# Second layer of a two-layer mixer kernel on one core: the pool half of the input projection taken on row differences

## The chip, the cores and the metric

The kernel runs on one core of one Trainium2 chip. The metric is the device time of one execution in microseconds (us), median of several runs. The engines are TensorE (PE in the profile; PEld are its weight loads), VectorE (DVE), ScalarE (ACT), GpSimd (POOL) and SyncE (SP), which issues the weight transfers.

## What is computed

Two layers act on 256 tokens (a grid of 4 rows of 64) with 2048 channels, all in float32. The first is a gated linear attention beside a short convolution. The second, which the change touches, is this (cut from the reference):

```
# layer 2: u = x * (1 + sc) + sh, with sc, sh, gt from w_ada
xp, gate = split(u @ w_in_o)                  # 2048 x 4096: a pool half and a gate half
xg = xp.reshape(4 rows, 64 columns, 2048)
z  = [window_mean_over_rows(g, w) - g for g, w in zip(4 groups of 512 channels, (2, 4, 8, 16))]
z  = [z_g @ w_pool[g] for each group] * pool_scale
y  = (z * silu(gate)) @ w_out_o
x  = layer_norm(alpha * x + gt * y)
```

With four rows only, the windows 8 and 16 cover all rows, so groups 2 and 3 both take the mean over the four rows minus the row. Every z is a combination of the differences of neighbouring rows.

## The kernel before

The tokens are two tiles of 128 (m = 0, 1). A float32 product is made of three products of parts: a weight tile w is split into a high part wh (ACT, line 153) and the rest wl (DVE, line 154), the activations likewise into u1h and u1l, and `mm3` (lines 189 to 193) adds uh·wh, uh·wl and ul·wh. Weights come in units of four contraction tiles by 512 columns, 1 MiB each, into four raw buffers in rotation; SP issues a load as soon as DVE has released the buffer (line 139). The split parts lie in four wh and four wl buffers, two units deep, which PE releases. `w_next` hands out the units in the order of the list `specs`, with loads two units and splits one unit ahead.

The second layer's input projection has eight blocks of 512 columns, four units each: x0 to x3 (the pool half, columns g*512) and g0 to g3 (the gate half, D + g*512). The order is x0, g0, p0, x1, g1, p1, x2, g2, p2, x3, g3, p3, where p is the group's 512x512 pool product, one unit. Each unit takes 4 contraction tiles x 2 token tiles x 3 products = 24 products of 128x512. After an x block, `pool_in` transposes it (zT, line 1200), forms z from sums of rows on DVE (lines 1208 to 1226) and splits it into zh and zl (lines 1230, 1231). After a p block DVE multiplies the sums in PSUM with the gate (line 1280), and `to_y1` transposes and splits the result (y1T, lines 1243 to 1248). The output projection (oacc) and the last normalisation follow.

Between the units runs background work. The gate gt of this layer is summed on DVE from 16 loads of w_ada (tile aacc, lines 528 and 530: four instructions a load), 0.55 steps a unit, and each fourth sum goes through a product with ones on PE (gtb, line 517). `x1_gen` applies the first normalisation's scale and shift to the residual (line 1171, eight instructions of 128x1024). The start of the layer is special: x0 goes token tile by token tile (`gemm_by_tile`), so that m = 0 is at work while the first layer's normalisation of m = 1 (`to_u1`, lines 1145 to 1157, tiles xr, xT, uf, u1h, u1l) still runs. Two units of x0 are split early; the other two lie in buffers of their own (swh, swl).

A scheduler turns this into one fixed order of instructions for each engine; each engine then works through its own order and waits where its next instruction is not ready.

Of the kernel before, what the change touches and what calls it, by code (L numbers as in the profile page):

```python
# [17 lines left out]
P = 128  # L18
# [31 lines left out]
TILE_1 = 4  # L50
# [11 lines left out]
def kernel(  # L62
# [96 lines left out]
    # units in the order of their use; loads and splits run ahead of the products  # L159
# [71 lines left out]
    # columns 2, 3: silu of c and c_ctx; a window of 32 columns puts them on the rows 0, 1 or 2, 3 of a product  # L231
# [5 lines left out]
    # columns of colT: see the rows above  # L237
# [26 lines left out]
    def mod_rows(k0, n):  # L264
        """scale (rows 0, 1 of each group of 32) and shift (rows 2, 3) of n channel tiles, summed over every fourth contraction tile"""
# [173 lines left out]
    def v_fill(nb, kt, nk):  # L439
        """a part of the values' contraction, for the gaps that the loads leave"""  # L440
# [34 lines left out]
    def ada_unit(layer, k0, n0):  # L475
        """four contraction tiles of the modulation's weights, two slots of two"""
# [26 lines left out]
    def ada_rows_gen(layer, dst, engs):  # L503
        """the gate of a layer, on every partition: products on DVE, the sum over the channels with ones"""
# [27 lines left out]
    def ada_cols_gen(layer, n0, dst, bias, one, engs, on_pe=()):  # L532
        """a section as channel columns: products on DVE, or on PE for the column blocks in on_pe"""
# [88 lines left out]
    def gemm_by_tile(groups, getu, done, budget=0.0, between=None, halves=False):  # L622
        """one token tile behind the other: the first one's sums are done while the second is at work"""
# [21 lines left out]
    # masks over (key j, query i) of a block of 32: m <= (j xor i) < 2 m  # L645
# [28 lines left out]
    def to_channels(nat, dst, use_act):  # L674
        """nat: two token tiles with 128 * n columns; dst(ct) for pairs of channel tiles"""
# [122 lines left out]
    def gla_gen(hp):  # L798
# [19 lines left out]
        def scores(xk, xq, flip=0):  # L818
            """keys of a block of 32 against the queries of the same block, or of its neighbour"""
# [52 lines left out]
        # chunk of 64 against the next one, tile of 128 against the other  # L872
# [108 lines left out]
    def rsqrt_act(v):  # L981
        """1 / sqrt(v + EPS): logarithm and exponential, then a Newton step"""
# [8 lines left out]
    def rsqrt(v, scale):  # L991
        """1 / sqrt(scale * v + EPS) on DVE: a seed from the exponent bits, then Newton steps"""
# [75 lines left out]
    def ln_blocks(src, order, getu, res, gt, budget, after, before=None, between=None, halves=False):  # L1068
        """sums of residual and projection and their statistics; after(m, tiles, mean, variance) when token tile m is done"""
# [58 lines left out]
    u1h, u1l = [], []  # L1128
# [8 lines left out]
    def to_u1(m, rt, mean, var):  # L1137
        rstd = rsqrt_act(var)
        ms = slice(m * P, (m + 1) * P)
        for nb in range(4):  # L1140
            if m == 0:
                u1h.append(slot([P, 4, SEQ], F32R, "u1h"))
                u1l.append(slot([P, 4, SEQ], F32R, "u1l"))
            r = rt[nb][:, m, :]
# [4 lines left out]
            uf = slot([P, 4, P], F32, "uf")  # L1149
# [44 lines left out]
    def pool_in(g, xp):
        X = slot([P, 4, SEQ], F32, "X1")
        for c2 in range(0, 4, 2):
# [4 lines left out]
            nc.scalar.activation(X[:, c2 : c2 + 2, :], pt, AF.Copy, scale=0.5 if g == 0 else 1.0)  # L1201
# [4 lines left out]

        if g == 0:
            tt(out=R(z, 0), in0=R(X, 0), in1=R(X, 0), op=ALU.subtract)
            tt(out=R(z, 1, 3), in0=R(X, 0, 3), in1=R(X, 1, 3), op=ALU.subtract)
        else:  # L1210
            sa = slot([P, 4, P], F32, "sa")
            a_, b_ = sa[:, :, 0:64], sa[:, :, 64:128]
            tt(out=a_, in0=R(X, 0), in1=R(X, 1), op=ALU.add)
            tt(out=b_, in0=R(X, 2), in1=R(X, 3), op=ALU.add)
# [120 lines left out]
```

## Time and profile before

| | us |
|---|---|
| median of 3 runs (1014.5 to 1016.17) | 1014.81 |
| span of the profiled execution | 1014.8 |
| first layer's last normalisation, second layer's first product | about 700 |
| second layer's input projection and pools | about 700 to 914 |
| output projection, up to PE's last product | 914 to 1003.6 |
| last normalisation and store | 1003.6 to 1014.8 |

The span of the profiled execution is the median, so differences in the trace can be set against the median as they are. An engine's busy time says little for PE, whose products overlap in the record; the distance from one start to the next is the better measure. A wait is put down to what ended it.

### The profile page before, as it was taken

How to read it: one execution, taken by the hardware profiler on the slowest of the kernel's cores; microseconds unless marked ns; L12 is line 12 of the kernel's file. 1: busy time of each engine (PE TensorE's matmuls, PEld its weight loads, DVE VectorE, ACT ScalarE, POOL GpSimd, SP SyncE). 2: the span in 40 equal slices, each digit the busy share in tenths (PEclk: the TensorE clock that was granted, in tenths of full speed). 3: DMA queues.
4: the chain of work that ended last, by engine and by line, in shares of the span. 5: the costliest groups of instructions: out<-in, count | busy, mean ns of one | idle time of the engine just before them, and what ended most of it. 6: DMA issues, size and time to landing. Idle time of an engine off the chain costs nothing.

```text
span 1014.8 us, 14425 instructions
## 1 busy us (share of the span) xinstructions
PE 973.4 (96%) x5718; PEld 768.6 (76%) x5718; DVE 801.4 (79%) x1161; ACT 463.3 (46%) x629; POOL 24.0 (2%) x55
## 2 busy tenths in 40 slices
PE   5899999999999999989999999999999999999995
PEld 4566666778878877877878788887888887778885
DVE  1555556989996999699999879987769968576676
ACT  2422214365684775336563444446554454454340
POOL 2000000000000000000000000000100001000000
PEclk9999999999999999999999999999999999999998
DMA  9987899667786676757767897984887888877532
GB/s 264 327 264 261 284 289 331 203 226 254 249 298 243 199 258 219 258 171 249 245 213 248 290 322 253 323 315 170 292 308 233 277 267 277 284 268 257 175 121 83
DMA packets 150373, 255.45 MB, mean 252 GB/s; under 512 B 5079, under 2 KB 46721, under 8 KB 150305
## 3 DMA queue, kind: packets, MB, share of 16 engines
q1 hardware_dynamic: 146592, 245.13, 72.3%
q0 software_dynamic: 2896, 8.72, 2.7%
q8 instruction: 45, 0.74, 0.3%
q10 hardware_dynamic: 816, 0.68, 0.3%
q14 instruction: 24, 0.19, 0.0%
HBM read 252.41 MB, written 2.10 MB: 251 GB/s over the span
## 4 chain that ended last, share of the span: by engine, by line
PE 43%; DVE 31%; DMA 19%; issue 4%; ACT 3%; SPq 0%; DVEq 0%; ACTq 0%
DMA raw<-in_w_ada_dram 16%; DVE wl L154 11%; DVE aacc L530 8%; PE oacc L191 5%; PE oacc L193 5%; PE oacc L192 5%; PE xacc L193 4%; PE xacc L192 4%; PE xacc L191 4%; PE ada L275 2%; PE kacc L191 2%; PE kacc L193 2%; PE kacc L192 2%; PE pr L402 1%; DMA raw<-in_w_in_e_dram 1%
## 5 line engine op out<-in xcount | busy, mean ns | idle before, releaser
L153 ACT CAST wh<-raw 128x1024 fp32r<-128x1024 f32 (+1 forms) x250 | 257.8, 1044 | 252.6 <-PE xacc L193 97.8
L154 DVE TENSOR_TENSOR wl<-raw,wh 128x1024 fp32r<-128x1024 f32 (+1 forms) x250 | 297.9, 1211 | 40.6 <-ACT wh L153 38.1
L530 DVE SCALAR_TENSOR_TENSOR aacc<-raw,sil,aacc 128x512 f32<-128x512 f32 x240 | 179.5, 748 | 42.6 <-DMA raw<-in_w_ada_dram 38.7
L191 PE MATMUL xacc<-wh,uxh 128*128 128x512 f32 x384 | 152.6, 397 | 0.0
L193 PE MATMUL xacc<-wh,uxl 128*128 128x512 f32 x384 | 151.8, 395 | 0.0
L192 PE MATMUL xacc<-wl,uxh 128*128 128x512 f32 x384 | 150.3, 391 | 0.1
L192 PE MATMUL xacc<-wl,u1h 128*128 128x512 f32 x240 | 94.4, 393 | 3.2 <-DVE wl L154 3.0
L191 PE MATMUL xacc<-wh,u1h 128*128 128x512 f32 x240 | 95.2, 397 | 0.8 <-ACT u1h L1156 0.8
L193 PE MATMUL xacc<-wh,u1l 128*128 128x512 f32 x240 | 93.7, 391 | 0.0
L192 PEld LDWEIGHTS xacc<-wl,uxh 128*128 128x128 f32 x384 | 72.1, 188 | 16.2 <-DVE wl L154 1.0
L193 PEld LDWEIGHTS xacc<-wh,uxl 128*128 128x128 f32 x384 | 72.2, 188 | 15.3 <-issue 0.2
L191 PEld LDWEIGHTS xacc<-wh,uxh 128*128 128x128 f32 x384 | 72.1, 188 | 15.5 <-ACT wh L153 0.5
L422 DVE TENSOR_TENSOR knat<-kacc,knat 128x512 f32<-128x512 f32 x64 | 42.8, 686 | 34.5 <-PE kacc L193 34.3
L192 PEld LDWEIGHTS xacc<-wl,u1h 128*128 128x128 f32 x240 | 45.1, 188 | 16.0 <-DVE wl L154 6.1
L191 PEld LDWEIGHTS xacc<-wh,u1h 128*128 128x128 f32 x240 | 45.1, 188 | 11.2 <-ACT u1h L1156 1.3
L193 PEld LDWEIGHTS xacc<-wh,u1l 128*128 128x128 f32 x240 | 45.1, 188 | 9.5 <-DVE u1l L1157 0.4
L286 ACT COPY arow<-ada 128x256 f32<-128x256 f32 (+1 forms) x9 | 3.1, 349 | 100.8 <-PE ada L275 100.8
L275 PE MATMUL ada<-raw,sil 128*32 128x256 f32 (+1 forms) x576 | 36.4, 382 | 10.8 <-DMA raw<-in_w_ada_dram 10.7
L191 PE MATMUL oacc<-wh,y1h 128*128 128x512 f32 (+1 forms) x120 | 45.5, 379 | 0.0
L193 PE MATMUL oacc<-wh,y1l 128*128 128x512 f32 (+1 forms) x120 | 45.0, 375 | 0.0
L192 PE MATMUL oacc<-wl,y1h 128*128 128x512 f32 (+1 forms) x120 | 45.0, 375 | 0.0
L275 PEld LDWEIGHTS ada<-raw,sil 128*32 128x32 f32 x576 | 17.3, 119 | 27.4 <-issue 12.6
(326 smaller groups left out, 1685.6 us busy)
## 6 DMA issues: line engine op xcount, KB each, us to landing
raw<-in_w_ada_dram SPq DMA_DIRECT2D x96, 1024.0 KB, 6.4
raw<-in_w_in_e_dram SPq DMA_DIRECT2D x54, 1024.0 KB, 5.7
raw<-in_w_in_o_dram SPq DMA_DIRECT2D x32, 1024.0 KB, 6.5
raw<-in_w_out_e_dram SPq DMA_DIRECT2D x16, 1024.0 KB, 7.0
raw<-in_w_out_o_dram SPq DMA_DIRECT2D x16, 1024.0 KB, 5.2
raw<-in_w_in_e_dram SPq DMA_DIRECT2D x18, 512.0 KB, 6.9
raw<-in_w_pool_dram SPq DMA_DIRECT2D x4, 1024.0 KB, 8.1
gt<-in_b_ada_dram POOLq DMA_DIRECT2D x8, 256.0 KB, 4.6
```

What stands on the lines that cost most here:

```text
L153: nc.scalar.copy(h, r[:, j : j + w, :])
L154: nc.vector.tensor_tensor(out=l, in0=r[:, j : j + w, :], in1=h.bitcast(F32), op=ALU.subtract)
L191: nc.tensor.matmul(out=acc, lhsT=uh, rhs=wh, start=start, stop=False)
L192: nc.tensor.matmul(out=acc, lhsT=uh, rhs=wl, start=False, stop=False)
L193: nc.tensor.matmul(out=acc, lhsT=ul, rhs=wh, start=False, stop=stop)
L275: nc.tensor.matmul(out=ps[32 * g : 32 * g + 32, :], lhsT=sil[:, kt, 2 - 2 * half : 34 - 2 * half], rhs=r[:, j, :], start=half == 0 and kt ...
L286: arow_ins.append(nc.scalar.copy(a[:, :nw], ps))
L402: nc.tensor.matmul(out=pr[32 * g : 32 * g + 32, :], lhsT=wr[:, kk, :], rhs=quad_u[kk // 2][:, kk % 2, :], start=True, stop=True,)
L422: nc.vector.tensor_tensor(out=dst, in0=acc, in1=dst, op=ALU.add)
L530: e.scalar_tensor_tensor(out=a, in0=r[j], scalar=sc, in1=a, op0=ALU.mult, op1=ALU.add)
```

## The change

A function `row_steps` runs after the first layer's normalisation. It forms the three differences of neighbouring rows of u (3 x 64 = 192 tokens), in tiles d, and splits them: dm0 and dm1 are the high part and the rest of the first two differences (128 tokens), dm2 holds the high part of the third difference in its first 64 tokens and its rest in the other 64. For this uf is kept whole (four tiles instead of eight short-lived ones).

An x block (`d_block`) now takes five products a contraction tile instead of six: dm0·wh, dm1·wh, dm0·wl into one accumulator, dm2·wh, dm2·wl into the other; the two halves of the latter are added after the transpose. `pool_in` forms z from the differences. The blocks stand in another order, written out in a list. A pool product that comes before its gate is copied out of PSUM by ACT (pooled) and multiplied when the gate is there. The whole program is instruction for instruction the same up to the normalisation at the start of the second layer. The diff, cut to its core:

```
-    for g in range(4):
-        if g == 0:
...
+    ODD = ("g0", "x0", "x1", "p0", "x2", "p1", "x3", "p2", "g1", "p3", "g2", "g3")
+    for s in ODD:
+        g = int(s[1])
+        if s == "g0":
             wide.update(len(specs) + i for i in WIDE_1)
-        block(W_O, g * 512)
-        block(W_O, D + g * 512)
-        block(W_P[g], 0, (0,))
+        if s[0] == "p":
+            block(W_P[g], 0, (0,))
+        else:
+            block(W_O, (D if s[0] == "g" else 0) + g * 512)
...
-            uf = slot([P, 4, P], F32, "uf")
+            uf = ufs[nb][:, :, ms]
...
+    def row_steps():
+        for nb in range(4):
+            if nb % 2 == 0:
+                dms.append([slot([P, 8, P], F32R, f"dm{i}") for i in range(3)])
+            dh, dl, dx = (t[:, 4 * (nb % 2) : 4 * (nb % 2) + 4, :] for t in dms[-1])
+            d = slot([P, 4, 192], F32, "d")
+            uf = ufs[nb]
+            nc.vector.tensor_tensor(out=d, in0=uf[:, :, 64:256], in1=uf[:, :, 0:192], op=ALU.subtract)
+            for hi, lo, src in ((dh, dl, d[:, :, 0:128]), (dx[:, :, 0:64], dx[:, :, 64:128], d[:, :, 128:192])):
+                nc.scalar.copy(hi, src)
+                nc.vector.tensor_tensor(out=lo, in0=src, in1=hi.bitcast(F32), op=ALU.subtract)
...
+    def d_block(n0, evac):
+        accs = [acc_bank("xacc") for _ in range(2)]
+        for q in range(4):
+            parts = w_next((W_O, 4 * q, 4, n0))
+            for j in range(4):
...
+                nc.tensor.matmul(out=accs[0], lhsT=dh, rhs=wh, start=f, stop=False)
+                nc.tensor.matmul(out=accs[0], lhsT=dl, rhs=wh, start=False, stop=False)
+                nc.tensor.matmul(out=accs[1], lhsT=dx, rhs=wh, start=f, stop=False)
+                nc.tensor.matmul(out=accs[0], lhsT=dh, rhs=wl, start=False, stop=l)
+                nc.tensor.matmul(out=accs[1], lhsT=dx, rhs=wl, start=False, stop=l)
...
         if g == 0:
-            tt(out=R(z, 0), in0=R(X, 0), in1=R(X, 0), op=ALU.subtract)
-            tt(out=R(z, 1, 3), in0=R(X, 0, 3), in1=R(X, 1, 3), op=ALU.subtract)
+            nc.gpsimd.memset(R(z, 0), 0.0)
+            nc.vector.tensor_copy(R(z, 1, 2), R(X, 0, 2))
+            tt(out=R(z, 3), in0=e2, in1=R(X, 3), op=ALU.add)
...
+            tt(out=e2, in0=e2, in1=R(X, 3), op=ALU.add)
...
+                stt(out=R(z, 0), in0=e1, scalar=2.0, in1=e2, op0=ALU.mult, op1=ALU.add)
+                stt(out=R(z, 0), in0=e0, scalar=3.0, in1=R(z, 0), op0=ALU.mult, op1=ALU.add)
+                for r, e in enumerate((e0, e1, e2)):
+                    stt(out=R(z, r + 1), in0=e, scalar=-4.0, in1=R(z, r), op0=ALU.mult, op1=ALU.add)
...
+            if g in gates1:
+                for m in range(2):
+                    tt(out=gates1[g][:, m, :], in0=accs[m], in1=gates1[g][:, m, :], op=ALU.mult)
+                later.append(lambda g=g: to_y1(g, gates1[g]))
+            else:
+                pooled[g] = slot([P, 2, 512], F32, "pooled")
+                for m in range(2):
+                    nc.scalar.copy(pooled[g][:, m, :], accs[m])
         else:
...
+            o_block(D + g * 512, gate_evac(g))
+            if g in pooled:
+                tt(out=gates1[g], in0=gates1[g], in1=pooled[g], op=ALU.mult)
+                later.append(lambda g=g: to_y1(g, gates1[g]))
```

Where the fixed orders move is seen at three places. The first is DVE at the end of the normalisation of m = 1. Before, after the rest u1l_3 of the third channel quarter come the splits of the two late units of the first block (raw_175 and raw_176):

```order
L1157 TENSOR_TENSOR u1l_1_5902<-uf_5_6047,u1h_1_5901 128x4x128
L1157 TENSOR_TENSOR u1l_2_5917<-uf_6_6060,u1h_2_5916 128x4x128
L1157 TENSOR_TENSOR u1l_3_5932<-uf_7_6073,u1h_3_5931 128x4x128
L1155 TENSOR_SCALAR uf_8_6086<-xT_8_6081,A1_5244,B1_5245 128x128
L154 TENSOR_TENSOR swl_9_6097<-raw_175_5977,swh_9_6096 128x1024
L154 TENSOR_TENSOR swl_10_6101<-raw_175_5977,swh_10_6100 128x1024
L1157 TENSOR_TENSOR u1l_4_5947<-uf_8_6086,u1h_4_5946 128x4x128
L154 TENSOR_TENSOR swl_11_6107<-raw_176_6104,swh_11_6106 128x1024
```

Changed, DVE at the same place (d_1 is the first quarter's difference; raw_177 and raw_178 are the first two units of x0, the second block now):

```order
L1175 TENSOR_TENSOR d_1_6092<-uf_1_5903 128x768
L1161 TENSOR_TENSOR u1l_2_5917<-uf_2_5918,u1h_2_5916 128x4x128
L1161 TENSOR_TENSOR u1l_3_5932<-uf_3_5933,u1h_3_5931 128x4x128
L1159 TENSOR_SCALAR uf_4_5948<-xT_8_6078,A1_5244,B1_5245 128x128
L153 TENSOR_TENSOR wl_159_6261<-raw_177_6140,wh_159_6260 128x1024
L1178 TENSOR_TENSOR dm1_1_6090<-d_1_6092,dm0_1_6089 128x512
L153 TENSOR_TENSOR wl_160_6265<-raw_177_6140,wh_160_6264 128x1024
L1161 TENSOR_TENSOR u1l_4_5947<-uf_4_5948,u1h_4_5946 128x4x128
L153 TENSOR_TENSOR wl_161_6269<-raw_178_6142,wh_161_6268 128x1024
L153 TENSOR_TENSOR wl_162_6273<-raw_178_6142,wh_162_6272 128x1024
L1178 TENSOR_TENSOR dm2_1_6091<-d_1_6092,dm2_1_6091 128x4x64
```

The late units of the first block have moved behind all of the row steps and behind two units of the next block.

The second place is DVE while PE is in x2: the product of gate 0 with the first pool product. Before, DVE comes to it between the next two splits after p0:

```order
L154 TENSOR_TENSOR wl_169_6415<-raw_185_6378,wh_169_6414 128x1024
L154 TENSOR_TENSOR wl_170_6419<-raw_185_6378,wh_170_6418 128x1024
L1280 TENSOR_TENSOR gate_1_6231<-pacc_1_6412,gate_1_6231 128x512
L154 TENSOR_TENSOR wl_171_6454<-raw_187_6422,wh_171_6453 128x1024
L1280 TENSOR_TENSOR gate_1_6231<-pacc_2_6413,gate_1_6231 128x512
```

Changed, DVE at that product: it stands behind three units of x2 (raw_192, raw_194, raw_195) and the z of the second group:

```order
L153 TENSOR_TENSOR wl_184_6748<-raw_195_6715,wh_184_6747 128x1024
L1255 SCALAR_TENSOR_TENSOR z_2_6632<-X1_2_6619 128x4x64
L1256 SCALAR_TENSOR_TENSOR z_2_6632<-X1_2_6619 128x4x64
L1257 TENSOR_TENSOR z_2_6632<-z_2_6632,X1_2_6619 128x4x64
L1259 TENSOR_SCALAR z_2_6632<-z_2_6632 128x4x64 x3
L533 SCALAR_TENSOR_TENSOR aacc1_14_6541<-raw_193_6646,sil_106,aacc1_14_6541 128x512
L1317 TENSOR_TENSOR gate_1_6121<-pacc_1_6583,gate_1_6121 128x512
L1268 TENSOR_TENSOR zl_2_6643<-z_2_6632,zh_2_6642 128x1024
```

PE reads that gate (y1T) inside x2's last unit.

The third place is the product gtb_6 with ones. Before, PE comes to it at the end of the first unit of g1:

```order
L193 MATMUL xacc_34_6873<-wh_188_6839,u1l_1_5902 128x512
L1243 MATMUL y1T_3_6910<-ident_79,gate_2_6652 128x128 x4
L1243 MATMUL y1T_4_6919<-ident_79,gate_2_6652 128x128 x4
L517 MATMUL gtb_6_6928<-aacc1_14_6560,ones_136 128x512
L191 MATMUL xacc_33_6872<-wh_189_6874,u1h_2_5916 128x512
```

Changed, PE inside the third unit of x3, and DVE at the last step of the sum aacc1_14 that this product reads:

```order
L1221 MATMUL xacc_33_6875<-wh_192_6914,dm0_2_6104 128x512
L1222 MATMUL xacc_33_6875<-wh_192_6914,dm1_2_6105 128x512
L1223 MATMUL xacc_34_6876<-wh_192_6914,dm2_2_6106 128x512
L520 MATMUL gtb_6_6907<-aacc1_14_6541,ones_136 128x512
L1224 MATMUL xacc_33_6875<-wl_192_6915,dm0_2_6104 128x512
```

```order
L153 TENSOR_TENSOR wl_193_6950<-raw_202_6918,wh_193_6949 128x1024
L153 TENSOR_TENSOR wl_194_6954<-raw_202_6918,wh_194_6953 128x1024
L533 SCALAR_TENSOR_TENSOR aacc1_14_6541<-raw_199_6803,sil_106,aacc1_14_6541 128x512
L1264 SCALAR_TENSOR_TENSOR z_3_6860<-X1_3_6847,z_3_6860 128x4x64
```

On DVE the step stands behind the split of x3's fourth unit (raw_202), while PE asks for it inside the third.

## Rows read from the trace of the kernel before

**Rows 1.** Page, span and part 1: engine busy us (share) x instructions.

```profile
span 1014.8 us, 14425 instructions
PE 973.4 (96%) x5718; PEld 768.6 (76%) x5718; DVE 801.4 (79%) x1161; ACT 463.3 (46%) x629; POOL 24.0 (2%) x55
```

**Rows 2.** Busy time by stretch: start:end length, engines, granted clock, DMA share, GB/s.

```profile
430.00:435.00 5.00, 1.37 (x7) 0.84 (x6) 4.48 (x20) 0.79 (x1) 0.00 (x0) 1.00 0.68 212
435.00:440.00 5.00, 5.00 (x16) 3.63 (x15) 4.42 (x7) 1.85 (x3) 0.00 (x0) 0.66 0.00 0
711.00:903.00 192.00, 188.95 (x847) 153.05 (x845) 148.78 (x180) 89.79 (x108) 9.59 (x18) 1.00 0.82 277
769.00:803.00 34.00, 33.49 (x151) 27.12 (x150) 32.87 (x40) 16.52 (x19) 1.06 (x2) 1.00 0.78 259
```

**Rows 3.** Waits of PE, 690 to 1015 us: total, times, longest.

```profile
PE xacc L192 <- DVE wl L154: 3.0, 5, 1.1
PE xacc L191 <- ACT u1h L1156: 0.8, 1, 0.8
```

**Rows 4.** Waits of PE, 430 to 440 us.

```profile
PE yT L965 <- DVE y L959: 3.6, 1, 3.6
```

**Rows 5.** Order of time on PE: start, us, what.

```profile
695.54 1.06 PE L1148 MATMUL xT<-ident,xr 128*128 128x128 f32 x8
...
708.47 0.50 PE L191 MATMUL xacc<-wh,u1h 128*128 128x512 f32 x1 [0.83 <-ACT u1h L1156]
...
711.60 0.39 PE L191 MATMUL xacc<-wh,u1h 128*128 128x512 f32 x1
711.83 0.39 PE L191 MATMUL xacc<-swh,u1h 128*128 128x512 f32 x1
712.05 0.39 PE L192 MATMUL xacc<-wl,u1h 128*128 128x512 f32 x1
...
967.63 0.39 PE L192 MATMUL oacc<-wl,y1h 128*128 128x512 f32 x1
...
969.89 0.39 PE L193 MATMUL oacc<-wh,y1l 128*128 128x512 f32 x1
```

**Rows 6.** Groups on DVE, 711 to 903 us: busy, mean ns, idle before.

```profile
L154 DVE TENSOR_TENSOR wl<-raw,wh 128x1024 fp32r<-128x1024 f32 x61 | 72.7, 1218 | 6.9 <-ACT wh L153 6.6
L530 DVE SCALAR_TENSOR_TENSOR aacc<-raw,sil,aacc 128x512 f32<-128x512 f32 x56 | 41.9, 749 | 25.4 <-DMA raw<-in_w_ada_dram 24.5
L528 DVE TENSOR_SCALAR aacc<-raw,sil 128x512 f32<-128x512 f32 x4 | 1.9, 486 | 10.7 <-DMA raw<-in_w_ada_dram 10.7
```

**Rows 7.** Order of time on DVE: back-to-back distances of each shape.

```profile
708.45 0.69 DVE L1157 TENSOR_TENSOR u1l<-uf,u1h 128x512 fp32r<-128x512 f32 x1
...
711.49 2.52 DVE L154 TENSOR_TENSOR swl<-raw,swh 128x1024 fp32r<-128x1024 f32 x2 [0.21 <-ACT swh L153]
...
733.11 0.42 DVE L1208 TENSOR_TENSOR z<-X 128x256 f32<-128x256 f32 x1
733.44 0.95 DVE L1209 TENSOR_TENSOR z<-X 128x768 f32<-128x768 f32 x1
...
740.92 2.35 DVE L154 TENSOR_TENSOR wl<-raw,wh 128x1024 fp32r<-128x1024 f32 x2
743.20 0.74 DVE L530 SCALAR_TENSOR_TENSOR aacc<-raw,sil,aacc 128x512 f32<-128x512 f32 x1
743.86 2.35 DVE L154 TENSOR_TENSOR wl<-raw,wh 128x1024 fp32r<-128x1024 f32 x2
749.03 3.11 DVE L530 SCALAR_TENSOR_TENSOR aacc<-raw,sil,aacc 128x512 f32<-128x512 f32 x4 [2.82 <-DMA raw<-in_w_ada_dram]
```

**Rows 8.** Waits of SP's load queue, 690 to 1015 us.

```profile
SPq L139 <- DVE wl L154: 175.2, 42, 9.1
```

**Rows 9.** Groups on ACT, 711 to 903 us.

```profile
L153 ACT CAST wh<-raw 128x1024 fp32r<-128x1024 f32 x63 | 65.6, 1052 | 62.9 <-PE xacc L193 49.2 <-issue 4.4 <-PE pacc L193 3.4
L1264 ACT COPY xp<-xacc 128x512 f32<-128x512 f32 x6 | 3.5, 584 | 5.7 <-PE xacc L193 5.7
```

More of the change, by code (lines that the diff above doesn't have):

```diff
@@ L1205, in R @@
             return t[:, :, 64 * r : 64 * (r + n)]
+        e0, e1, e2 = (R(X, r) for r in range(3))
+        ts = nc.vector.tensor_scalar
         if g == 0:
-            tt(out=R(z, 0), in0=R(X, 0), in1=R(X, 0), op=ALU.subtract)
-            tt(out=R(z, 1, 3), in0=R(X, 0, 3), in1=R(X, 1, 3), op=ALU.subtract)
-        else:
[L1211 to L1214, printed above, removed]
+            nc.gpsimd.memset(R(z, 0), 0.0)
+            nc.vector.tensor_copy(R(z, 1, 2), R(X, 0, 2))
+            tt(out=R(z, 3), in0=e2, in1=R(X, 3), op=ALU.add)
+        else:
+            tt(out=e2, in0=e2, in1=R(X, 3), op=ALU.add)
@@ L1236, in to_y1 @@
         yl = slot([P, 4, SEQ], F32R, "y1l")
-        y1h.append(yh)
-        y1l.append(yl)
+        y1h[g], y1l[g] = yh, yl
         for c2 in range(0, 4, 2):
@@ L1248, in to_y1 @@
                 stt(out=yl[:, cc, :], in0=pt[:, j, :], scalar=wcol, in1=hq.bitcast(F32), op0=ALU.mult, op1=ALU.subtract)
-    for g in range(4):
-        if g == 1:
-            bg.append(x1_gen())
-        xp = slot([P, 2, 512], F32, "xp")
-        rest, gaccs = (0, 1, 2, 3), None
-        if g == 0:
-            accs = [acc_bank("xacc") for _ in range(2)]
-            groups = [(W_O, 0, (0, 1, 2, 3), accs, True)]
-            if TILE_1 > 4:
-                gaccs = [acc_bank("xacc") for _ in range(2)]
-                groups.append((W_O, D, tuple(range(TILE_1 - 4)), gaccs, False))
-                rest = tuple(range(TILE_1 - 4, 4))
-            gemm_by_tile(groups, getu_1, lambda m, cs, end: nc.scalar.copy(xp[:, m, :], accs[m]), budget=B)
-        else:
-            o_block(g * 512, lambda m, a: nc.scalar.copy(xp[:, m, :], a))
-        later.append(lambda g=g, xp=xp: pool_in(g, xp))
-        gate = slot([P, 2, 512], F32, "gate")
-        def gate_evac(m, a):
-            last_silu[0] = nc.scalar.activation(gate[:, m, :], a, AF.Silu)
-        o_block(D + g * 512, gate_evac, rest, gaccs)
-        accs = [acc_bank("pacc") for _ in range(2)]
-        def getz(m, kt):
-            s = slice(m * P, (m + 1) * P)
-            return zs[g][0][:, kt, s], zs[g][1][:, kt, s]
-        gemm(w_pool[0, g], 0, (0,), range(2), getz, accs, budget=B)
-        for m in range(2):
-            tt(out=gate[:, m, :], in0=accs[m], in1=gate[:, m, :], op=ALU.mult)
-        later.append(lambda g=g, gate=gate: to_y1(g, gate))
@@ new lines, with gate_evac, f, getz @@
+    gates1, pooled = {}, {}
+    def gate_evac(g):
+        gates1[g] = slot([P, 2, 512], F32, "gate")
+        def f(m, a):
+            last_silu[0] = nc.scalar.activation(gates1[g][:, m, :], a, AF.Silu)
+        return f
+    for s in ODD:
+        g = int(s[1])
+        if s == "g0":
+            accs = [acc_bank("xacc") for _ in range(2)]
+            f = gate_evac(0)
+            gemm_by_tile([(W_O, D, (0, 1, 2, 3), accs, True)], getu_1, lambda m, cs, end: f(m, accs[m]), budget=B)
+        elif s[0] == "x":
+            xp = slot([P, 2, 512], F32, "xp")
+            d_block(g * 512, lambda m, a: nc.scalar.copy(xp[:, m, :], a))
+            later.append(lambda g=g, xp=xp: pool_in(g, xp))
+            if g == 0:
+                bg.append(x1_gen())
+        elif s[0] == "p":
+            accs = [acc_bank("pacc") for _ in range(2)]
+            def getz(m, kt):
+                c = slice(m * P, (m + 1) * P)
+                return zs[g][0][:, kt, c], zs[g][1][:, kt, c]
+            gemm(w_pool[0, g], 0, (0,), range(2), getz, accs, budget=B)
+            if g in gates1:
[4 more added lines that the diff above has]
+                pooled[g] = slot([P, 2, 512], F32, "pooled")
+                for m in range(2):
+                    nc.scalar.copy(pooled[g][:, m, :], accs[m])
+        else:
+            o_block(D + g * 512, gate_evac(g))
+            if g in pooled:
+                tt(out=gates1[g], in0=gates1[g], in1=pooled[g], op=ALU.mult)
+                later.append(lambda g=g: to_y1(g, gates1[g]))
```

41 lines of the change are left out of this document (21 added, 20 removed).

## The prediction, made before the changed kernel ran

> **What bounds the kernel now.** I read the page first, then the stretches of the second layer, then the waits of PE, then DVE. The page gives PE 96% of the span [rows 1]; that alone is not enough, since products overlap in the record. The measure is the distance between starts: from 967.63 to 969.89 us ten products of 128x512 start, 0.226 us each, with no gap [rows 5]. In the second layer's input projection (711 to 903 us) PE is busy 188.95 of 192 us at full clock [rows 2], and between 690 and 1015 us it waits only 3.8 us in all, of which 3.0 us are waits for a split wl on DVE [rows 3]. So PE sets the end, and a product taken from it should be worth 0.226 us. But the second engine is close behind: DVE is busy 148.78 of the same 192 us [rows 2], and 43 us of its idle time are waits: 36.1 us in front of aacc for loads of w_ada, 6.9 us in front of a split [rows 6]. SP waits 175.2 us for DVE to give raw buffers back, 42 times [rows 8], so loads start when DVE has finished a buffer, and DVE stands still when the next load has not landed. The five waits of PE for wl [rows 3] are the places where this loop already was no faster than PE. ACT is far from its limit: 89.79 of 192 us [rows 2], and 49.2 us of the idle time in front of its casts are waits for PE [rows 9].
>
> **What is removed.** The pool half has 4 blocks of 16 contraction tiles. Six products a tile are 384, five are 320: 64 products less, 64 x 0.226 = **14.5 us** off PE. Weights, loads and splits of weights are the same in number. That two accumulators alternate costs nothing by the trace: at 711.60, 711.83 and 712.05 us products into different accumulators start 0.225 us apart [rows 5].
>
> The Trainium skill (TensorE: Matmul & The Clock Gate, Part 2) gives the gap of back-to-back products of 512 columns as 215.7 ns at full clock. By that price the 64 products would be worth 13.8 us, 0.7 us less; the trace's own distance, 226 ns, is used here.
>
> **What is added.** On DVE, per channel quarter, one difference of 768 elements (0.95 us alone, about 0.87 back to back), a rest of 512 (0.69, about 0.60) and one of 256 (0.42, 0.33) [rows 7]: four times 1.8 us are 7.2 us. The new pool_in is about 1 us shorter in all: for the first group a copy of 512 and a sum of 256 replace 256 and 768 elements, for the second ten short steps replace nine, three of them cheap scalings; groups 2 and 3 are even. The gates come out even too. DVE gains about 6 us of work. ACT gets eight casts (four of 512, four of 256 elements) and six copies of 128x512 at 0.58 us [rows 9], some 7 us, hidden by its 102 us of idle time; if that cover went, each would delay a cast of weights by as much.
>
> **The start of the layer.** The order puts x0's first unit and the row steps in front of the late units of g0. PE resumes at 708.47 us with m = 1 [rows 5]; 24 products later, at 713.9, it wants the first differences, and 12 products after that, at 716.6, the first dm2. On DVE, from 711.5 us, when before it began swl_9 [rows 7], stand four splits (1.14 each), two 512s (0.60) and one 256 (0.33) up to the rest of dm2: 6.1 us, so 717.6. PE waits 1.0 us there, and a further 0.3 to 0.5 us at x0's second quad, whose differences follow on DVE at 719 to 720.3. I take **1.4 us**; the ends are 0 (DVE gets there as PE does) and 4 us (one more load or cast late).
>
> **The x stretch.** This term decides. From 711.5 us up to the last step of aacc1_14, which gtb_6 reads, DVE has in its order 40 splits x 1.14 = 45.4 us, 32 aacc at 0.66 to 0.78 [rows 7], 22.4 us, eight xr of the splits' shape, 9.1 us, and 16.4 us of small ones (row steps, z, zl, gates, y1l): 93.3 us. Without idle time it would be done at 804.8. PE has 414 products (93.6 us) and 32 transposes (1.06 us for eight [rows 5], 4.2 us) from 708.47 to gtb_6, and the 1.4 us: 807.7. So DVE has only 2.9 us to spare, against 93.3 of work. The gate product in front of y1T is the same case a little earlier: its first half falls at 711.5 + 70 = 781.7, PE arrives near 784. Every microsecond that DVE is idle beyond about 3 is lost on PE. In the stretch 769 to 803, where DVE had xr, z and splits to do at once, it was busy 32.87 of 34 us, idle 3.3% [rows 2]; over all of 711 to 903 it was idle 22.5%, much of it while PE set the pace. Over 93 us of work these give 3 and 27 us of idle time. The load here is nearer the first row, but the loads of w_ada go on, which in the first row were far ahead. I take 8 us, so PE loses 8 - 2.9 = about **5 us**; the ends are 0 and 24 us.
>
> A long wait has a second price. When PE waited 3.6 us at 430 us [rows 4], its granted clock was 0.66 over the next 5 us [rows 2], as if 3.4 of them ran at 1.2 instead of 2.4 GHz: 1.7 us. I count that **once**, with ends 0 and 3.4.
>
> **The rest.** From g1 on, units take PE 24 x 0.226 = 5.4 us again, the supply's pace of before. About half of the 3.0 us of waits for wl lay in units that are now in the x stretch, counted anew there; so **-1.5 us** (ends -3 and 0). The output projection is left as it is: [rows 3] lists all waits of PE up to the end, and none is in oacc. What is late next is DVE, not ACT or DMA: in 711 to 903 the DMA engines moved 277 GB/s at 0.82 of their time [rows 2].
>
> **Sum**, against the profiled execution, which is as long as the median: 1014.8 - 14.5 + 1.4 + 5 + 1.7 - 1.5 = 1006.9. I say **1006.9 us**, 0.8% less.
>
> **Rivals.**
> 1. The full gain. DVE is idle for no more than 3 us in the x stretch, as in 769 to 803. Then 1014.8 - 14.5 + 1.4 - 1.5 = 1000.2; with one short wait 1001 to 1003. For it: DVE ran 34 us on end almost without a gap [rows 2]. Against: the loads of w_ada stood between, and an aacc in DVE's order waits for its load in front of all splits behind it [rows 6].
> 2. The supply takes what PE gives. DVE idles 16 us (17%) in the x stretch, since a unit of x leaves the loop 20 x 0.226 = 4.5 us instead of 5.4. Then PE loses 13, the sum is 1014.8 - 14.5 + 1.4 + 13 + 1.7 - 1.5 = 1014.9: no change. For it: the five waits for wl already there at 5.4 us a unit [rows 3].
> 3. Slower. DVE idles as in the whole stretch, 22.5%, 27 us. PE then loses 24 in waits at the gate and gtb and in front of splits, at least two of them followed by half clock (3.4): 1014.8 - 14.5 + 1.4 + 24 + 3.4 - 1.5 = 1027.6. It decides from about 18 us of idle time on. For it: the row itself, over 192 us; against: that idle time arose while DVE's splits waited for ACT and ACT for PE, which a DVE that is behind does not do.
> 4. The products do not get cheaper in step, because dm2, a tile of two kinds of halves, or the alternation raises the distance: at 0.25 us instead of 0.226 the 320 products cost 7.7 us more, 1014.6. Rows 5 speak against it.
>
> The Trainium skill (TensorE: Matmul & The Clock Gate, HAM oscillation) describes kernels in which every group of products starts at half rate after a wait for data; by that rule each of rival 3's long waits would pay the second price, and the trace agrees once, with 0.66 after 3.6 us.
>
> **How the numbers follow.** Forecast (DVE idle for 4 to 12 us, 1003 to 1011) 0.62; full gain 0.15; supply takes it 0.12, spread over 1011 to 1015.5; slower 0.08; dearer products 0.03. A measurement of this kernel can tell about 0.2%, 2 us, from no change: faster is below 1012.8, slower above 1016.8. Faster: 0.62 + 0.15 + 0.05 of rival 2 + 0.01 = 0.83. Same: 0.07 + 0.02 = 0.09. Slower 0.08. The range reaches 1001.5 to 1013.5: it leaves out the best third of the full gain (0.05), the worst half of rival 2 (0.06) and rival 3 (0.08).
>
> **What would show it.** Right: about 5650 products on PE; a first x block's products at 0.226 us; a wait of PE of about 1 us for a row step near 717; waits for the gate or for aacc in front of y1T and gtb_6 of some microseconds in all; DVE busy over 85% between 711 and 810. The first g1 product should start near 827 us. Wrong: DVE idle there as before (rivals 2 and 3 show waits for wl at every unit of x), a distance above 0.23 us (rival 4), or a wait above 4 us at the late units of g0, where swl_9 and swl_10 come after all row steps. If the start costs more than 4 us, my walk through DVE's order is wrong there.

## The result, and the profile after

The changed kernel takes 1006.82 us (median of 6 runs, 1005.23 to 1012.59) beside 1017.53 us (1014.5 to 1019.9) for the kernel before on the same chip: a ratio of 0.9898, 95% interval 0.9875 to 0.9921. Timed a second time (last experiment below) it took 1009.77 beside 1017.04, 0.992 (0.9896 to 0.9945). The forecast was 1006.9 us. The total came out, closer than its terms: some of them were wrong, and 10 us were left in the kernel.

The page of the profiled execution, span and busy time by engine:

```profile
span 1004.1 us, 14346 instructions
PE 958.9 (95%) x5654; PEld 757.0 (75%) x5654; DVE 807.0 (80%) x1172; ACT 468.9 (47%) x643; POOL 24.4 (2%) x56
```

Against [rows 1] the 64 products are gone (5718 to 5654), DVE has 5.6 us more, and the span is 10.7 us shorter. But not all of that is the change. Up to the point where PE resumes with the second token tile (m = 1) in the second layer's first block, both programs do the same work. In [rows 5] that is at 708.47 us; here, in order of time on PE:

```profile
432.69 0.41 PE L968 MATMUL yT<-ident,y 128*128 128x128 f32 x2 [1.95 <-DVE y L962]
...
704.54 0.50 PE L190 MATMUL xacc<-wh,u1h 128*128 128x512 f32 x1 [0.83 <-ACT u1h L1160]
```

PE is there 3.9 us sooner. Of these, 3.4 come from one place: it waited 1.95 us instead of 3.63 [rows 4], and its clock did not fall, as the stretch shows (columns as in [rows 2]: the seventh column is the granted clock):

```profile
435.00:440.00 5.00, 5.00 (x24) 4.24 (x23) 5.00 (x11) 2.78 (x7) 0.00 (x0) 1.00 0.36 98
```

So I measure what follows by the **length of the layer**: span less the start of that product. Before: 1014.8 - 708.47 = 306.3 us; after: 1004.1 - 704.54 = 299.6, which is 6.8 us less, not 10.7 and not 14.5. Where the other 7.7 us went stands in the waits of PE from 690 to 1005 us (total, times, longest), to be read beside [rows 3]:

```profile
PE y1T L1279 <- DVE gate L1326: 3.3, 1, 3.3
PE xacc L1221 <- ACT wh L152: 2.5, 1, 2.5
PE y1T L1279 <- DVE gate L1317: 1.1, 1, 1.1
PE xacc L190 <- ACT u1h L1160: 0.8, 1, 0.8
PE xacc L1223 <- DVE dm L1178: 0.6, 1, 0.6
PE xacc L191 <- DVE wl L153: 0.4, 1, 0.4
PE gtb L520 <- DVE aacc L533: 0.3, 1, 0.3
PE pacc L191 <- DVE wl L153: 0.3, 1, 0.3
PE xacc L1224 <- DVE wl L153: 0.3, 1, 0.3
```

Without the 0.8 us that both kernels have, these are 8.8 us against 3.0 before, 5.8 us more. After the longest, the clock fell over 5 us:

```profile
880.00:885.00 5.00, 1.69 (x11) 1.19 (x10) 3.69 (x5) 1.82 (x2) 0.00 (x0) 1.00 0.57 188
885.00:890.00 5.00, 5.00 (x19) 4.01 (x17) 4.85 (x7) 1.78 (x4) 0.00 (x0) 0.66 0.77 249
```

That costs 0.34 x 5 = 1.7 us of products; 5.8 + 1.7 = 7.5 of the 7.7. Three waits make most of it.

**743 us.** ACT's cast stood 9.01 us in front of a load that SP had issued at 731.08 and that took 11.1 us. On POOL's queue six loads of `x1_gen`, 256 KB each, had been issued from 728.22 to 731.47, while SP's weight loads ran. Order of time on ACT, then on POOL, then a stretch (DMA share and GB/s are the last two columns):

```profile
742.26 1.99 ACT L152 CAST wh<-raw 128x1024 fp32r<-128x1024 f32 x2 [9.01 <-DMA raw<-in_w_in_o_dram]
```

```profile
728.22 0.54 POOL L1184 DMA_DIRECT2D row<-in_ln_g_dram  x1 [3.58 <-PE xacc L192]
...
731.47 0.54 POOL L1184 DMA_DIRECT2D row<-in_ln_b_dram  x1
```

```profile
735.00:745.00 10.00, 7.20 (x31) 5.34 (x30) 4.46 (x6) 2.02 (x3) 0.00 (x0) 1.00 1.02 371
```

The share alone is no proof: without the rows it is as high (experiment 9, 1.04 over the same stretch). What differs is whose bytes they are. From 728 to 743 us the rows took 1.57 MB (q0, POOL's queue) beside 3.53 of weights (q1, SP's); in experiment 9, 729 to 744 us, weights took all 5.24, and such a load landed in 7.2 us. Packets, MB and share of the 16 engines, changed kernel first:

```profile
q1 hardware_dynamic: 1782, 3.53, 64.0%
q0 software_dynamic: 480, 1.57, 37.2%
...
q1 hardware_dynamic: 2638, 5.24, 99.4%
```

The rows' 1.57 MB at 371 GB/s are 4.2 us by estimate, and the load took 3.9 us longer. (The Trainium skill, DMA: Bandwidth & Descriptors, Queues, rings and completion order, says that each DMA engine goes round the queues it has work for, a packet at a time. Experiment 9 fits that; no run here shows the packets in turn.) The rows are not the only condition. In experiment 4 they went out at the same times, but the load had been issued at 724.58 us instead of 731.08, and PE did not wait.

**785 us.** DVE has done the eight xr steps of the same generator, 1.22 us each, between 759 and 775 us, and the gate's product, which PE waits for, comes behind them:

```profile
766.32 3.49 DVE L1191 TENSOR_TENSOR xr<-xr,row 128x1024 f32<-128x1024 f32 x3
...
784.37 0.74 DVE L533 SCALAR_TENSOR_TENSOR aacc<-raw,sil,aacc 128x512 f32<-128x512 f32 x1
785.03 0.68 DVE L1317 TENSOR_TENSOR gate<-pacc,gate 128x512 f32<-128x512 f32 x1
```

**881 us.** DVE stands 4.46 us in front of a step of the gate sum whose load has not landed; a split and the gate's product, whose inputs ACT had finished at 880.8 and 877.2 us, are queued behind it:

```profile
881.28 0.75 DVE L533 SCALAR_TENSOR_TENSOR aacc<-raw,sil,aacc 128x512 f32<-128x512 f32 x1 [4.46 <-DMA raw<-in_w_ada_dram]
881.95 1.22 DVE L153 TENSOR_TENSOR wl<-raw,wh 128x1024 fp32r<-128x1024 f32 x1
883.08 1.22 DVE L1326 TENSOR_TENSOR gate<-gate,pooled 128x1024 f32<-128x1024 f32 x1
```

### The profile page after: what moved, and what is told of

It is laid out like the page before. It is cut to its first block, busy times and chain, and to the rows that moved or that the text cites. A ratio compares the mean times of both kernels' runs of the same rounds, so it can differ in the third digit from the quotient of the medians.

```text
span 1004.1 us, 14346 instructions
## 1 busy us (share of the span) xinstructions
PE 958.9 (95%) x5654; PEld 757.0 (75%) x5654; DVE 807.0 (80%) x1172; ACT 468.9 (47%) x643; POOL 24.4 (2%) x56
## 4 chain that ended last, share of the span: by engine, by line
PE 49%; DVE 29%; DMA 15%; issue 4%; ACT 2%; SPq 0%; DVEq 0%; ACTq 0%
DMA raw<-in_w_ada_dram 12%; DVE wl L153 10%; DVE aacc L533 7%; PE oacc L190 5%; PE oacc L191 5%; PE oacc L192 5%; PE xacc L192 5%; PE xacc L191 5%; PE xacc L190 5%; PE ada L274 2%; DMA raw<-in_w_in_o_dram 2%; PE kacc L190 2%; PE kacc L192 2%; PE kacc L191 2%; PE pr L405 1%
## 5 line engine op out<-in xcount | busy, mean ns | idle before, releaser
L190 PE MATMUL xacc<-wh,u1h 128*128 128x512 f32 x112 | 44.9, 401 | 0.8 <-ACT u1h L1160 0.8
L191 PE MATMUL xacc<-wl,u1h 128*128 128x512 f32 x112 | 44.7, 399 | 0.5 <-DVE wl L153 0.4
L192 PE MATMUL xacc<-wh,u1l 128*128 128x512 f32 x112 | 44.5, 397 | 0.0
L190 PE MATMUL kacc<-wh,uxh 128*128 128x512 f32 x64 | 26.8, 418 | 1.5 <-ACT uxh L397 1.5
L1221 PE MATMUL xacc<-wh,dm 128*128 128x512 f32 x64 | 25.7, 402 | 2.5 <-ACT wh L152 2.5
L190 PE MATMUL kacc<-wh,uch 128*128 128x512 f32 x64 | 26.4, 412 | 0.5 <-DVE knat L425 0.5
```

The source lines that it names most:

```text
L190: nc.tensor.matmul(out=acc, lhsT=uh, rhs=wh, start=start, stop=False)
L191: nc.tensor.matmul(out=acc, lhsT=uh, rhs=wl, start=False, stop=False)
L192: nc.tensor.matmul(out=acc, lhsT=ul, rhs=wh, start=False, stop=stop)
L1221: nc.tensor.matmul(out=accs[0], lhsT=dh, rhs=wh, start=f, stop=False)
```

## The experiments

All times are medians; the layer's length is from one profiled execution as above (two of one kernel differ by 0.7 us before and 2.4 us after). The scheduler orders DVE anew in each kernel, so an edit moves more than its own lines.

| kernel | us | ratio to before (95%) | layer, us | waits of PE that matter, us |
|---|---|---|---|---|
| before | 1017.5 | | 306.3 | wl 3.0 in five |
| before again | 1015.9 | 0.9996 (0.9979 to 1.0013) | 305.6 | wl 2.3 in five |
| changed | 1006.8 | 0.9898 (0.9875 to 0.9921) | 299.6 | 2.5, 1.1, 3.3 |
| changed again | 1009.8 | 0.9920 (0.9896 to 0.9945) | 297.2 | 2.2, 1.1, 2.9 |
| six products | 1023.6 | 1.0079 (1.0060 to 1.0099) | 311.7 | 3.4 at y1T, wl 2.4 |
| old order, five | 1005.9 | 0.9908 (0.9893 to 0.9924) | 297.5 | wl 2.5, zl 2.2 |
| quarter sum | 1001.3 | 0.9866 (0.9845 to 0.9886) | 293.9 | 3.1 at y1T, wl 1.3 |
| no row steps | 1009.6 | 0.9943 (0.9921 to 0.9966) | | 4.6 and 2.7 at y1T |
| rows late | 1008.3 | 0.9914 (0.9892 to 0.9936) | 297.7 | 4.4 and 2.0 at y1T |
| sum behind gate | 1004.7 | 0.9876 (0.9849 to 0.9903) | 292.4 | 2.1 at 746, 0.9 at y1T |
| gate first | 1007.2 | 0.9915 (0.9888 to 0.9943) | 299.5 | 2.9, and 3.7 at y1T |
| xr later | 1007.7 | 0.9899 (0.9870 to 0.9928) | 296.3 | 5.3 in two at y1T |
| three moves | 1003.5 | 0.9857 (0.9834 to 0.9880) | 293.6 | 3.2 at y1T |
| xr behind gate | 997.3 | 0.9800 (0.9775 to 0.9824) | 287.7 | none over 0.8 |

**1. Before again.** No edit.

> The kernel before, unchanged, profiled once more. In the two profiles so far the second half of the last output block of layer 1 resumes at 708.47 us (before) and 704.54 us (after), although both programs are the same up to there; the difference of 3.9 us lies at 430 us, where PE waited 3.6 us for y and then ran at a granted clock of 0.66 (before), against 2.0 us and full clock (after). Theory: that is chance, not the change; this profile shows either kind, a span between 1010.5 and 1015 us, and the timed runs stay at 1014 to 1020. Rival: the change reaches back in some way; then this profile shows 3.6 us and 0.66 at 430 again, and 708.5.

PE waited 2.58 us at 435.21 us, the clock stayed at 1.00, and the resume came at 706.74 us. Theory: part of the 10.7 us between the first two profiles is chance. In the thirteen profiles that have the row (the resume with m = 1) it lies between 704.2 and 710.4 us; the changed kernel alone has 704.5 and, profiled again, 710.3, and the kernel before lies between, at 708.5 and 706.7.

**2. Six products again**, order and row steps kept (the added product counts one term twice):

```
-                nc.tensor.matmul(out=accs[1], lhsT=dx, rhs=wl, start=False, stop=l)
+                nc.tensor.matmul(out=accs[1], lhsT=dx, rhs=wl, start=False, stop=False)
+                nc.tensor.matmul(out=accs[1], lhsT=dx, rhs=wh, start=False, stop=l)
```

> The changed kernel with a sixth product in each of the 64 contraction tiles of the pool half: the product of the third difference with the high part stands twice (its sum counts that term twice). Order, differences, splits and loads stay. Theory 1 (PE sets the end, and some 4 us of the waits in the x stretch, 2.8 at 743, 1.1 at 785 and 0.3 us for the gate's sum, come from DVE being short there): the 64 products cost 14.5 us and those waits go, so 10 to 14.5 us more than the changed kernel's 1006.8: 1017 to 1021. Rival (the x stretch runs at the pace of loads and splits, products are hidden in waits): 0 to 5 us more, 1007 to 1012.

The layer is 12.1 to 14.5 us longer than the changed kernel's two (311.7 less 299.6 or 297.2): theory 1, PE sets the end, and the 64 products are worth nearly all of their 14.5 us. The median, 1023.6, is above the 1017 to 1021 expected, 16.8 and 13.8 us above the changed kernel's two medians. One part of theory 1 failed: the wait at the gate, 1.1 us in the changed kernel, did not go but grew to 3.4 us (at 793.29 us), with clocks of 0.68 and 0.63 over 790 to 800 us. The second finding: with as many products as before the layer is 5.4 to 6.1 us longer than before's two. That is the price of the new order and the row steps.

**3. Old order, five products**, no differences:

```
+        if five[0] and m == 1:
+            nc.tensor.matmul(out=acc, lhsT=uh, rhs=wh, start=start, stop=False)
+            nc.tensor.matmul(out=acc, lhsT=uh, rhs=wl, start=False, stop=stop)
+            return
...
+        five[0] = n0 < D
         gemm(W_O, n0, quads, range(2), getu_1, accs, first=first, budget=B)
+        five[0] = False
```

> The kernel before with its order of blocks and without any differences, but one of the six products of the pool half left out in all 64 contraction tiles (the low part of the second token tile, so that part of the sum is missing). It shows what the removal of products alone is worth. Theory 1: PE sets the end and DVE has no row steps and no blocks of five products back to back, so 12 to 14.5 us come off the 1017.5 of before: 1003 to 1005.5, 2 to 4 us under the changed kernel; what the changed kernel lost against 14.5 us is then the price of its row steps and its order. Rival: the supply of split weights takes it in the old order too: 8 us or less, 1009.5 or more.

The edit reached three blocks of the pool half only, 48 products and not 64, since x0 is written by another routine; 48 are worth 10.9 us. The layer became 8.1 to 8.8 us shorter; the median, 1005.9, is just above the 1003 to 1005.5 expected for 64. So the old order, without a row step, also lost 2 to 3 us, to a wait for zl and two for wl: part of the supply rival is true in either order.

**4. Quarter of the gate sum:** three of four steps are left out.

```
-                ada_accum(ada_unit(layer, k0, n0), k0, a, engs)
+                ada_accum(ada_unit(layer, k0, n0), k0, a, engs, 1 if layer else 4)
...
-            for j in range(4):
+            for j in range(n):
```

> The changed kernel with three of every four multiply steps of the layer-1 gate sum left out (48 of 64, some 33 us of DVE); the loads of w_ada stay. Theory 1 (DVE's work is what is short): the waits of PE for the gate at 785 and 881 us and for the gate's sum go, 5 to 8 us less: 999 to 1002. Rival (loads are short, not work): the first step of a unit still stands in DVE's order ahead of the gate and waits for its load, as 4.5 us at 877 to 881 us in the changed kernel; PE's waits at 743 and 881 us stay, 0 to 2 us less: 1005 to 1007.

The time is theory 1's, its mechanism is half wrong: the waits at 743 and 881 us went, but the one in front of the first y1T stayed and grew (at 781.81 us, 3.1 us):

```profile
PE y1T L1279 <- DVE gate L1317: 3.1, 1, 3.1
```

The gate's product came 4.1 us sooner than in the changed kernel (780.98 us, not 785.03), but PE asked for it 6.0 us sooner (778.8, not 784.8): the wait at 743 us was no longer ahead of it, and the xr steps still stood ahead of the gate, from 755 to 771 us.

**5. No row steps:** the five products read u1h and u1l.

> The changed kernel without the row differences: the five products of a tile read the tiles of layer 1's output as they are (so the pool half is not the differences' product), and DVE and ACT have none of the row steps, 7 us on DVE. Number and order of products, blocks, loads and splits stay. Theory 1 (the row steps push the splits of the late units of the first gate block back, buffers come free later, and the load that PE waits for at 743 us starts late): PE's waits at 713 (0.6 us) and 743 us (2.5 us) go, with the products' slow restart behind them some 4.5 us: 1002 to 1003 against 1006.8. Rival (the wait at 743 us comes from the order, six loads that share the DMA engines from 726 us on): it stays, and only the 1 us at 713 goes: 1005.5 to 1006.

Both missed. The wait at 743 us went, as theory 1 says, but the time is 1009.6, above the changed kernel's first median (1006.8) and level with its second (1009.8). PE now stood 4.58 us at the first y1T (795.37 us), with a clock of 0.83 over 790 to 800, and 2.66 us at a later one (895.15 us). This profile has no resume row; the eight xT ahead of it start at 702.33 us, against 691.63 and 697.35 in the changed kernel's two. From there to the end it is 311.0 us, against 312.5 and 310.2: no gain. By the same clock PE came to the first y1T 4.7 us sooner than in the changed kernel's first profile and the gate's product only 1.2 us sooner, so the same deadline was missed by more.

**6. Rows late:**

```
-    row_steps()
+    row_steps(0, 2)
+    later.append(lambda: row_steps(2, 4))
```

> The changed kernel with the row steps of channel quarters 2 and 3 written behind the first gate block and x0's first unit, so that the splits of the late gate units come first on DVE; nothing is left out. Theory 1 (as in the run without row steps): splits end some 3.5 us earlier, buffers come free earlier, PE's wait of 2.5 us at 743 us shrinks or goes: 2 to 3.5 us less, 1003 to 1005. Rival: the late differences hold up x0's third unit, a wait for a difference of 1 to 4 us takes the place: 1006 to 1009.

The wait at 743 us fell from 2.5 to 0.6 us, theory 1, and more than that came back at the first gate, which neither text had named (the median, 1008.3, is the rival's):

```profile
PE y1T L1280 <- DVE gate L1318: 4.4, 1, 4.4
```

After it the clock over 790 to 795 us was 0.51.

**7. Sum behind the gate:** the sum's steps are held over the last two units of g1 to g3 and issued behind the gate's product.

```
-        with prio(ADA_PRIO):
+        with prio(ADA_PRIO), (tc.issue_after(gate_ins[-1].ins) if gate_ins else nullcontext()):
...
+        held[0] = True
+        gemm(W_O, n0, HOLD[1], range(2), getu_1, accs, first=False, budget=B)
+        held[0] = False
```

> The changed kernel with the steps of the layer-1 gate sum held back over the last two units of g1, g2 and g3 and placed behind the gate's product on DVE; nothing is left out. Theory 1 (at 877 to 881 us DVE stood 4.5 us in front of a step of the sum whose load had not landed, with a split and the gate's product queued behind it, and PE waited 3.3 us for that, then ran at a granted clock of 0.83 over 880 to 890 us): both go, 4 to 5 us less, 1002 to 1003. Rival: the steps that come later hold up a split behind them; waits for wl of the same size appear after the gate, 1005.5 to 1008.

Theory 1: the wait at 881 us and the slow stretch went, no wait for wl took their place, and the layer is 292.4 us, 4.8 to 7.2 us shorter. The median, 1004.7 (998.0 to 1007.3), is above the 1002 to 1003 expected; it carries the scatter from before the layer, and the waits at 746 and 789 us stayed.

**8. Gate first:**

```
+                with prio(-GATE_PRIO):
+                    for m in range(2):
+                        tt(out=gates1[g][:, m, :], in0=accs[m], in1=gates1[g][:, m, :], op=ALU.mult)
```

> The changed kernel with the product of gate and pooled values moved ahead in DVE's order for g0 (by one or two splits and one step of the sum); nothing is left out. Theory 1 (the wait of 1.1 us in front of y1T at 785 us is DVE's order): it goes, 1 to 1.5 us less, 1005 to 1006. Rival (DVE is full there, busy 9.9 of 10 us): the wait moves to a split or to the gate's sum, within 0.5 us of the changed kernel, 1006.3 to 1007.3.

The rival's time with another mechanism: the wait at 785 us went; the one at 743 us (2.9 us) was followed by a clock of 0.66 over 745 to 750 us this time, which took the gain.

**9. xr later:**

```
-            if g == 0:
-                bg.append(x1_gen())
...
+            if g == 1:
+                bg.append(x1_gen())
```

> The changed kernel with the eight steps xr (residual times ln_g, plus ln_b; 9.1 us of DVE) written at g1 instead of behind x0; nothing is left out. In the changed kernel they stand on DVE from 759 to 775 us, ahead of the gate's product that PE waits for at 785 us. Theory 1 (what DVE has to do in the x stretch ahead of that gate decides the wait): with 9.1 us less there the wait in front of y1T goes, also in profiles where PE reaches it sooner, 1.5 us less by the changed kernel's profile and up to 5 us by the others': 1002 to 1005.5. The wait at 743 us stays. Rival (the gate waits for a chain of its own: product, cast, sum): the wait stays within 1 us of what it was, 1006 to 1008.

The wait at 785 us went, as theory 1 says; so did the one at 743 us, which it said would stay. The eight row loads of the same generator, 2 MB on POOL's queue, had moved with the steps, and the weight load issued at 732.03 us was there for the cast at 739.23, in 7.2 us instead of 11.1:

```profile
739.23 2.00 ACT L152 CAST wh<-raw 128x1024 fp32r<-128x1024 f32 x2 [4.99 <-DMA raw<-in_w_in_o_dram]
```

But the steps now stood ahead of g1's gate, and PE waited there, and again at the next one, so that the median, 1007.7, is the rival's:

```profile
854.15 1.06 PE L1279 MATMUL y1T<-ident,gate 128*128 128x128 f32 x8 [2.94 <-DVE gate L1326]
...
882.06 1.53 PE L1279 MATMUL y1T<-ident,gate 128*128 128x128 f32 x8 [2.33 <-DVE gate L1326]
```

**10. Three moves** (6, 7 and 9 together).

> Three moves together, nothing left out: xr steps at g1, row steps of channel quarters 2 and 3 behind the first gate block, steps of the gate sum behind the gate's product for g1 to g3. Theory 1 (the changed kernel's loss of 8 us against the pitch is three separate waits, at 743, 785 and 881 us with what follows each): PE's time beyond the pitch falls from 16.4 us to 8 to 10 us, as in the kernel before (8.5 and 7.8): 998 to 1001, the full 14.5 us. Rival (DVE is short over the whole layer and a wait that is cured comes back at the next place, as the run with late row steps shows at 790 us): 1003 to 1006.

The rival's time (1003.5), and its mechanism too: the three waits went, but one came at the next place, 3.2 us in front of g1's y1T, behind xr; the layer is 293.6 us.

**11. xr behind the gate:** as 10, with `x1_gen` started at g2 and its steps queued behind g1's gate product on DVE; nothing is left out.

```
+                with tc.issue_after(gate_ins[0].ins):
+                    nc.vector.tensor_tensor(out=rt[nb], in0=rt[nb], in1=t.unsqueeze(1).to_broadcast([P, 2, 512]), op=op)
...
+            if g == 2:
+                bg.append(x1_gen())
```

> As the three moves together, but the xr steps stand behind g1's gate product on DVE instead of ahead of it; nothing is left out. In the run before, xr ahead of that gate made PE wait 3.2 us in front of y1T at 850 us and run slow after it, 5.1 us together. Theory 1 (each wait is a matter of what stands ahead of the gate in DVE's order): that goes, PE's time beyond the pitch falls from 10.6 us to 5 to 7 us: 998 to 1000. Rival (DVE has no room there either): a wait of 2 to 4 us comes at g2's gate or at a split, 1002 to 1005.

Theory 1, and more: 997.25 us (995.2 to 1000.31), 2.0% under the kernel before and the best here. PE's waits from 690 us on, and the two halves of the layer:

```profile
PE xacc L191 <- ACT u1h L1166: 0.8, 1, 0.8
PE xacc L1234 <- DVE dm L1184: 0.6, 1, 0.6
PE xT L1158 <- issue: 0.2, 1, 0.2
```

```profile
711.00:810.00 99.00, 98.39 (x446) 80.47 (x445) 92.46 (x118) 59.41 (x76) 2.49 (x5) 1.00 0.86 298
810.00:903.00 93.00, 92.92 (x421) 76.58 (x420) 77.15 (x89) 47.09 (x57) 8.54 (x16) 1.00 0.92 315
```

The layer is 287.7 us: 18.6 and 17.9 less than before's two. The 14.5 of the products and before's 3.0 of waits are 17.5; the rest is about what those waits cost beyond their length (around 796.69 us before, ten starts behind 0.40 us of wait take 0.68 us longer than at 0.227), less the 0.6 still waited. DVE is busier from 711 to 810 us (92.46) than in the changed kernel (91.07), and PE waits for 0.6 us of it.

**12. The changed kernel again.** No edit.

> The changed kernel, unchanged, profiled and timed once more beside the version with three moves. Theory: the waits at 743, 785 and 881 us (2.5, 1.1 and 3.3 us in the first profile) stand in this one too, each within 1.5 us, since DVE's order is the same, and the time of PE beyond the pitch is 14 to 19 us of the layer; the time before the layer may be 0 to 6 us longer, by the wait for y near 430 us: median 1005 to 1009. Rival: the waits were chance; one or two of them are missing.

All three waits stood again, each within 0.4 us: they belong to the order. (The median, 1009.8, is a little above the 1005 to 1009 expected; the resume came at 710.3 us.) This time the clock stayed at 1.00 behind the 2.90 us at y1T, which is most of the 2.4 us between the two lengths.

## Why the prediction was right, and where it was not

- **Removal, 14.5 us.** Right. In x0 the products start evenly, in order of time on PE; 25 of them, with dm0, dm1 and dm2 and the two accumulators in turn, 24 distances in 5.44 us:

```profile
735.01 0.39 PE L1221 MATMUL xacc<-wh,dm 128*128 128x512 f32 x1
735.24 0.39 PE L1222 MATMUL xacc<-wh,dm 128*128 128x512 f32 x1
735.46 0.39 PE L1223 MATMUL xacc<-wh,dm 128*128 128x512 f32 x1
...
740.45 0.39 PE L1225 MATMUL xacc<-wl,dm 128*128 128x512 f32 x1
```

  0.227 us each, so rival 4 is out, and experiment 2 shows 12.1 to 14.5 us for all 64, its own waits included. The prediction's other estimate, 13.8 us, from the distance of 215.7 ns that the Trainium skill (TensorE: Matmul & The Clock Gate, Part 2) gives, lies inside that too; the distance itself is not what the trace has.
- **The start, 1.4 us.** The row-step wait came where the walk through DVE's order put it, 0.6 us at 713.9 (717.8 on before's clock), where 1.0 and another 0.3 to 0.5 were forecast. So the start cost less than 1.4, and inside its ends. What the walk left out hit later, at 743 us: it followed x1_gen's eight xr steps and not its eight row loads. They had been issued from 711.25 to 724.64 us before and are issued from 728.22 on now, onto the loads of x0's and x1's units; with the 0.3 us behind it that wait is 2.8 us, and it belongs to the next term.
- **The x stretch, 5 us.** Idle time and loss came out, the reason did not. DVE was busy 91.07 of the 99 us from 711 to 810, 7.9 idle where 8 were assumed, and PE's waits there beside the 0.6 are 2.5, 0.3, 1.1 and 0.3, 4.2 us. But 5.4 us of the idle time is one stand at 738 to 743 us for the late load, and experiments 4 and 5 took work from DVE without curing the gate. Wrong was the step "Every microsecond that DVE is idle beyond about 3 is lost on PE", drawn from 93.3 us of work up to gtb_6: work in that sum that nobody waits for there, 9.1 us of xr, stood ahead of the gate and could stand elsewhere. Experiments 9 to 11 show it; in 11 DVE is idle for 6.5 of the 99 us, and PE waits 0.6. (Where gtb_6 stood before is put wrongly above: at 812.43 us it follows the first unit of x2, not of g1.)
- **Half clock once, 1.7 us.** Right in number, 0.66 over 885 to 890 us, but at g2's gate and not in the x stretch.
- **The rest, -1.5 us.** Wrong in sign: from g1 on PE waited 0.7 us for wl and 3.3 in front of y1T, 4.0 us against before's 3.0. Its reason was a misreading too. It put about half of before's waits for wl into units that are now in the x stretch; all five lie in gate blocks, g1 (the first), g2 (two) and g3 (two):

```profile
796.69 0.50 PE L192 MATMUL xacc<-wl,u1h 128*128 128x512 f32 x1 [0.40 <-DVE wl L154]
...
842.16 0.50 PE L192 MATMUL xacc<-wl,u1h 128*128 128x512 f32 x1 [0.34 <-DVE wl L154]
...
848.76 0.50 PE L192 MATMUL xacc<-wl,u1h 128*128 128x512 f32 x1 [0.86 <-DVE wl L154]
...
884.48 0.50 PE L192 MATMUL xacc<-wl,u1h 128*128 128x512 f32 x1 [0.31 <-DVE wl L154]
...
903.14 0.50 PE L192 MATMUL xacc<-wl,u1h 128*128 128x512 f32 x1 [1.09 <-DVE wl L154]
```

  The wait in front of y1T did not come from the new order of PE's blocks alone: at least a unit of products lies on PE between the gate's last input and its y1T in both orders. It came because the gate's product stood on DVE behind a step of the sum without its load, as at 881 us above, and the text called the gates even on work without asking what stands ahead of them. Experiment 7 shows that wait curable.
- **Sum.** In the layer -7.9 us were forecast; -6.8 is the first pair of profiles, -6.0 to -9.1 all four pairs. The first g1 product started at 822.85, 826.8 us on before's clock, forecast 827. The timed medians give -10.4 and -8.1 us, by their ratios. That the median meets 1006.9 to 0.1 us is therefore luck. The sum starts from the span of a profile, 1014.8, which equalled the median of three runs; but every run with both numbers takes 1.7 to 1.9 us longer than its span, and with three more runs the median before is 1017.5. Rival 1 (full gain, 1000.2) is reached, and passed, only in experiment 11.

## What to carry to other kernels

When one engine is 90% busy, ask of each deadline what stands ahead of it in that engine's order and could stand behind it, before adding up its work: moving 9 us of xr and a few other steps was worth 10 us, while taking 7 us of work away gained nothing and taking 32 us away (experiment 4) gained 3 to 6. A step that is moved takes its loads along: 1.6 MB of rows on another queue made a weight load 4 us late. And compare two profiles from an event that both have before the change, here 3.9 of 10.7 us lay ahead of it.

## What was not expected of the hardware

The length of a wait alone does not tell whether the clock falls after it. Behind 2.94 us (experiment 9) it was 0.66 over 855 to 860 us, behind 2.90 us (experiment 12) it stayed at 1.00; behind the waits of 3.1 to 4.6 us in front of y1T it fell each time, but it also fell behind 2.33 us (experiment 9, 0.76 over 880 to 885 us) and not behind 2.66 (experiment 5). The first layer's part, the same work in every kernel, took 704.2 to 710.4 us; two stretches make most of that, 40 to 50 us (granted clock 0.66 in experiment 12, 1.00 in both first profiles) and 435 to 440 us (0.66 before, 0.71 in experiment 12, 1.00 after). The clock is not all of it: with 1.00 in both, the second profile of before took 706.7 us and experiment 4 704.2. What decides between the two clocks I did not try.
